# Projection matmuls in runs of twelve instead of six beside the attention of a hybrid decoder step

## The chip, the cores and the metric

The kernel runs on one core of a Trainium2 chip. The metric is the device time of one execution in microseconds (us), the median over runs. The names of the engines are those of the profile: PE (TensorE) multiplies, PEld is its weight load, DVE (VectorE) and ACT (ScalarE) do element work, POOL (GpSimd) does some of it too and issues gathers, and SP issues nearly all other transfers.

## The reference, cut to what matters

One layer of a decoder is applied to a prompt of 1024 tokens and to 8 samples of one token each:

```python
def adaln_project(x, c, w_ada, b_ada, w_in, b_in):
    mod = jax.nn.silu(c.astype(jnp.float32)) @ w_ada + b_ada
    shift, scale, gate = jnp.split(mod[:, None, :], 3, axis=-1)
    h = layer_norm(x) * (1.0 + scale) + shift
    split_points = np.cumsum(IN_SPLITS)[:-1].tolist()
    parts = jnp.split(h @ w_in + b_in, split_points, axis=-1)
    return parts, gate
...
        hm, (C_p, n_p, m_p) = mlstm_mixer(qm, km, vm, om, im, fm, m_norm_g[l], carry0, M_CHUNK)
        ha = nsa_prompt(qa, cmp_p, slc_p, win_p, ga, cmp_params, rel_bias)
        mix = jnp.concatenate([hm * jax.nn.silu(zm), ha * jax.nn.silu(za)], axis=-1)
        x_p = residual_out(x_p, mix, gate, w_out[l], b_out[l], ln_g[l], ln_b[l])
```

`h @ w_in` is the input projection: 1024 features in, 4384 out. Its outputs feed two groups of heads. The mLSTM group has 4 heads, each a chain of 8 chunks of 128 tokens. The attention group (NSA) has 8 query heads over 2 shared key/value heads and three branches: compressed blocks, selected blocks (16 of the 16 that a prompt has, so all that are causal) and a window of 512. For the samples the selected blocks come from a paged cache. The output projection follows, then a residual with a layer norm.

## The kernel before, in words

The order of all instructions is fixed when the program is built. Work is written as Python generators, called lanes. A lane emits instructions up to its next `yield`. `Lanes.run` then picks the lane of lowest rank whose operands are ready by a clock that the planner keeps (class `Plan`), and where none is ready it takes the one that is ready soonest. Each engine runs its own part of that fixed order and waits by semaphores.

The lanes that matter here, by rank:

- `all_scores` (rank 0) and `all_values` (rank 1): the attention of the prompt in 32 units (key/value head, block of 128 queries, pair of heads). The second key/value head goes through its query blocks from the longest to the shortest, so the last units are small. A unit has score products (PE: `sc<-kst,qs` and `sc<-kst,ql`), minima on DVE, exponentials on ACT, nine small steps in `factors` on DVE and ACT, scaling on ACT or DVE (`pp<-pp,ef`; `pa`, `pw` in the longer units), transposes on PE (`tp<-KA,pp`), copies on ACT or DVE (`pt<-tp`) and value products on PE (`oo<-pt,VT`, `oo<-pt,vcp`).
- `mlstm_prep`, `mlstm_head`, `mlstm_norm` (rank 2): per head two groups of four chunks. A chunk has three products (`sc<-vx,kw`, `sc<-cx,qm`, `sc<-vx,wt`); a group ends with a norm whose reciprocal root runs in small steps on POOL (`rs_v` to `mva`) and with four transposes (`tp<-KA,nd`).
- `sample_mlstm` (rank 5), `out_weights` (rank 6): after the attention and the third chain input of head 3, the state update of the samples (`Cst`), and then the output weights (`wof` times the gate, split into `woh` and `wol`). `output` needs all of these.
- `projections` (rank 9): 35 blocks of 128 output features, in the order of `order`. It is the last choice, and so it fills what the others leave free.

`in_proj` emits one block: three column chunks of 344 tokens, eight feature blocks `k` of 128 for each, three matmuls for each `k` (`mm<-hh,wh`, `mm<-hl,wh`, `mm<-hh,wl`). I call the three matmuls of one `k` a step, and number the steps through all blocks: block 28 has steps 673 to 696. After every second `k` it yields, and so six matmuls stand in a run:

```python
                if k % 2:
                    yield 0
```

The blocks of the mLSTM have a gate of their own. Block 29 (`qm`, head 3) is not begun before head 2 has ended, or before all attention values have, whichever is first:

```python
                if t:
                    yield from done("next%d" % (t - 1))
```

`flags` holds the names of what has ended; `PARTS` are the five flags "parts0" to "parts4" of the samples' selected rows and window rows. They are all set when some 304 of the 840 steps have been emitted.

Of the kernel before, what the change touches and what calls it, by code (L numbers as in the profile page):

```python
# [354 lines left out]
def build(ctx, tc, I, O, dbg=None):  # L355
# [5 lines left out]
    flags = lanes.flags  # L361
# [32 lines left out]
    def bank(tag, hold=False):  # L394

        def first():
            return min(idle(b) for b in range(8))
        if first() > plan.clock["PE"]:
            yield first
        while first() >= BIG:  # L400
            yield first
        return take(tag, hold)

    def free(*banks):

        for t in banks:
            held[next(b for b in range(8) if owner[b] is not None and owner[b].tensor.name == t.tensor.name)] = False
# [483 lines left out]
    def w_fetch(i):  # L891
        if i >= len(order):
            return
        name, t = order[i]
        wf = wfs[i] = R([128, 8, 128], "wf")
        if name == "g":
            dma(wf[:, :, 0:32], I["w_gate"].rearrange("p (k c) -> p k c", k=8))
        else:
            dma(wf.rearrange("p k c -> p (k c)"), I["w_blk"][BLOCKS.index((name, t))])

    def w_split(i):
        if i >= len(order):
            return
        wf = wfs.pop(i)
        wh, wl = [R([128, 8, 128], x, F32R) for x in ("wh", "wl")]
        n = 32 if order[i][0] == "g" else 128
        split(wh[:, :, 0:n], wl[:, :, 0:n], wf[:, :, 0:n])
        if n == 32:
            V.tensor_copy(wh[:, :, 32:64], fb(wl)[:, :, 0:32])
        whl[i] = (wh, wl)  # L910
# [10 lines left out]
    def done(*names):  # L921

        for n in names:
            if n not in flags:
                yield n
# [45 lines left out]
    def in_proj(i, evac, then=None):  # L971

        def later(wait, ev):
            yield wait
            yield from ev

        def last():
            yield from done(*["ev%d_%d" % (i, x) for x in range(3)])
            then()
        wh, wl = whl.pop(i)  # L980
        w_fetch(i + 1)
        for x, (c0, w) in enumerate(CH):
            if i == 0 and x:
                yield from done("h%d" % (x + 1), *(["hs"] if x == 2 else []))
            ps = yield from bank("mm", True)
            m = slice(c0, c0 + w)
            for k in range(8):
                if order[i][0] == "g":

                    T.matmul(ps[0:64, 0:w], wh[:, k, 0:64], hh[k][:, m], start=(k == 0), stop=False)  # L990
                    T.matmul(ps[0:64, 0:w], wh[:, k, 0:64], hl[k][:, m], start=False, stop=(k == 7))
                else:
                    T.matmul(ps[:, 0:w], wh[:, k], hh[k][:, m], start=(k == 0), stop=False)
                    T.matmul(ps[:, 0:w], wh[:, k], hl[k][:, m], start=False, stop=False)
                    T.matmul(ps[:, 0:w], wl[:, k], hh[k][:, m], start=False, stop=(k == 7))
                if k % 2:
                    yield 0
            ev = evac(ps[:, 0:w], c0, w)
            if ev:
                lanes.add(ER, later(next(ev), ev), "ev%d_%d" % (i, x))  # L1000
            free(ps)
            if x == 0:
                w_split(i + 1)
        if then:
            lanes.add(ER, last())
# [430 lines left out]
    PARTS = ["parts%d" % i for i in range(5)]  # L1436
# [449 lines left out]
    def projections():  # L1886
# [7 lines left out]
        for i, (name, t) in enumerate(order):  # L1894
            j = TI.get(name, 0) + t
            b, bh = BT[:, j:j + 1], BTH[:, j:j + 1]
            if name == "g":
                def evg(ps, c0, n):
                    low = H([32, 344], "gl")
                    S.activation(low, ps[32:64], AF.Identity, bias=bg)  # L1900
                    V.tensor_tensor(GT[:, c0:c0 + n], ps[0:32], low, op=ALU.add)
                yield from in_proj(i, evg)
                lanes.add(2, gates(), "gates")
            elif name == "qa":
                q = R([128, NT], "qt")
                yield from in_proj(i, plain(q, b))
                lanes.add(2, q_done(t, q), "q%d" % t)
                if t == 0:
                    lanes.add(4, ada(2))
            elif name == "za":  # L1910
# [10 lines left out]
                def z_done(t=t, z=z):  # L1921
                    V.tensor_copy(SZS[:, t], z[:, SEQ:NT])
                    store(gtd[4 + t], z[:, 0:SEQ], "z%d" % t)
                yield from in_proj(i, evz2, z_done)
            elif name in ("ck", "cv", "sk", "sv", "wk", "wv"):
                f = R([128, NT], "kvf")
# [544 lines left out]
```

## Time and profile before

| what | us |
|---|---|
| median of 3 runs | 1038.01 |
| their range | 1035.63 to 1041.17 |
| the profiled execution, its own time | 1039.46 |
| its span from first to last instruction | 1037.6 |
| PE busy | 959.7 |
| DVE busy | 717.2 |
| ACT busy | 530.2 |
| POOL busy | 286.5 |

Busy times are of the profiled execution. A matmul's recorded length overlaps that of the next one, so what one matmul costs is read from the distance between two starts. The granted clock is given as a share of full speed: 1.00 is 2.4 GHz, 0.50 is 1.2 GHz.

### The profile page before, as it was taken

To read this page: it belongs to the slowest core of one execution; us is meant where nothing else is said; L and a number is where in the kernel's file an instruction comes from. 1 tells how busy PE (TensorE), PEld (TensorE's weight loads), DVE (VectorE), ACT (ScalarE), POOL (GpSimd) and SP (SyncE) were. 2 spreads that over 40 slices of the span, in tenths; PEclk is the share of its full clock that TensorE was granted. 3 is DMA by queue.
4 is the path that set the end of the run, shared out by engine and by line. 5 is a ranking of instruction groups with operands and counts; after the bars stand their busy time and mean duration, and the time that the engine had idled before them with its cause. 6 is when DMAs were issued, how large, how long until landed. Compare 5 with 4: busy or idle time off the path is not lost.

```text
span 1037.6 us, 20058 instructions
## 1 busy us (share of the span) xinstructions
PE 959.7 (92%) x7338; PEld 864.9 (83%) x7338; DVE 717.2 (69%) x2266; ACT 530.2 (51%) x1329; POOL 286.5 (28%) x362
## 2 busy tenths in 40 slices
PE   4997899999999989999999999999999899989990
PEld 3786897989888889899999998899998889967780
DVE  4859864072323477789777788878784738999996
ACT  3557752143344656676667786666773321231111
POOL 6216423111453000110131001131012524253563
PEclk9988899999999989999999999999999989989996
DMA  8943419413698715311105111012102326479502
GB/s 329 408 189 117 148 70 361 151 50 118 221 326 286 216 55 165 111 57 37 47 11 157 29 47 38 25 36 74 47 33 85 113 65 191 142 264 362 168 22 81
DMA packets 85334, 141.42 MB, mean 136 GB/s; under 512 B 11657, under 2 KB 58286, under 8 KB 85108
## 3 DMA queue, kind: packets, MB, share of 16 engines
q1 hardware_dynamic: 76020, 106.59, 31.2%
q0 software_dynamic: 9216, 33.56, 9.0%
q8 instruction: 58, 0.95, 0.4%
q14 instruction: 40, 0.33, 0.1%
HBM read 117.73 MB, written 28.15 MB: 141 GB/s over the span
## 4 chain that ended last, share of the span: by engine, by line
PE 57%; DVE 11%; DMA 4%; issue 2%; POOL 2%; ACT 1%; POOLq 0%; SPq 0%; DVEq 0%; ACTq 0%
PE mm L308 27%; PE sc L308 13%; PE tp L308 9%; PE oo L308 7%; DVE xr L308 2%; DMA wof<-in_w_out 1%; DMA pgs<-in_cache_slc_kv,idx 1%; DVE smp L308 1%; DVE lnst L308 1%; DVE rs_t L308 1%; POOL wol L308 1%; DMA mg<-mgd 1%; DVE mixl L308 1%; DMA pgs<-in_cache_win_kv 1%; DVE rs_y L308 0%
## 5 line engine op out<-in xcount | busy, mean ns | idle before, releaser
L308 PE MATMUL mm<-hh,wh 128*128 128x344 f32 (+1 forms) x840 | 286.3, 341 | 0.0
L308 PE MATMUL mm<-hl,wh 128*128 128x344 f32 (+1 forms) x840 | 270.4, 322 | 0.0
L308 PE MATMUL mm<-hh,wl 128*128 128x344 f32 x816 | 262.6, 322 | 0.0
L308 POOL TENSOR_TENSOR wl<-wf,wh 128x1024 fp32r<-128x1024 f32 (+1 forms) x35 | 82.5, 2356 | 505.0 <-ACT wh L308 389.6
L308 PEld LDWEIGHTS mm<-hh,wh 128*128 128x128 f32 (+1 forms) x840 | 158.8, 189 | 12.1 <-issue 10.5
L308 PEld LDWEIGHTS mm<-hl,wh 128*128 128x128 f32 (+1 forms) x840 | 158.9, 189 | 0.7
L308 PEld LDWEIGHTS mm<-hh,wl 128*128 128x128 f32 x816 | 155.1, 190 | 0.0
L308 PE MATMUL oo<-pt,VT 128*64 128x128 f32 x1056 | 70.1, 276 | 0.0
L308 PE MATMUL sc<-kst,qs 128*128 128x448 f32 (+6 forms) x208 | 69.5, 343 | 0.3 <-DVE pt L308 0.3
L308 PE MATMUL sc<-kst,ql 128*128 128x448 f32 (+6 forms) x208 | 65.5, 325 | 0.0
L308 PEld LDWEIGHTS oo<-pt,VT 128*64 128x64 f32 x1056 | 58.1, 137 | 6.4 <-issue 5.2
L308 DVE COPY pt<-tp 128x512 f32<-128x512 f32 (+1 forms) x87 | 54.8, 645 | 9.9 <-PE tp L308 9.7
L308 ACT ACTIVATE pw<-pw,nbs 128x64 f32<-128x64 f32 (+2 forms) x112 | 54.6, 489 | 12.6 <-DVE tot L308 6.4
L308 ACT ACTIVATE pt<-tp 128x512 f32<-128x512 f32 (+1 forms) x73 | 39.8, 558 | 40.6 <-PE tp L308 40.4
L308 ACT ACTIVATE pa<-pa,nbs 128x384 f32<-128x384 f32 (+1 forms) x88 | 50.9, 580 | 14.6 <-DVE pa L308 12.4
L308 ACT ACTIVATE xh<-tp 128x512 fp32r<-128x512 f32 x64 | 38.0, 595 | 35.2 <-PE tp L308 34.9
L308 DVE TENSOR_TENSOR xl<-tp,xh 128x512 fp32r<-128x512 f32 x64 | 42.8, 679 | 14.3 <-ACT xh L308 14.0
L308 PE MATMUL tp<-KA,pgx 128*128 128x128 f32 x256 | 43.3, 293 | 2.8 <-ACT pgx L308 1.9
L308 ACT ACTIVATE ti<-sc,PKT 128x129 f32<-128x129 f32 x28 | 10.3, 369 | 67.3 <-DVE cx L308 67.3
L308 ACT ACTIVATE pp<-pp,nbs 128x64 f32<-128x64 f32 (+3 forms) x72 | 32.2, 449 | 22.7 <-DVE nbs L308 21.3
L308 PE MATMUL sc<-xl,w1h 128*128 128x256 f32 x128 | 38.3, 299 | 5.0 <-DVE xl L308 5.0
L308 PEld LDWEIGHTS sc<-kst,qs 128*128 128x128 f32 x208 | 39.8, 191 | 3.3 <-DVE pt L308 1.0
(506 smaller groups left out, 2285.0 us busy)
## 6 DMA issues: line engine op xcount, KB each, us to landing
wf<-in_w_blk SPq DMA_DIRECT2D x34, 512.0 KB
wada<-in_w_ada SPq DMA_DIRECT2D x24, 512.0 KB
wof<-in_w_out SPq DMA_DIRECT2D x16, 512.0 KB
xt<-in_x_prompt SPq DMA_DIRECT2D x8, 512.0 KB
pgs<-in_cache_win_kv SPq DMA_DIRECT2D x8, 512.0 KB
qf<-qtd SPq DMA_DIRECT2D x32, 128.0 KB
mix<-mxd SPq DMA_DIRECT2D x16, 256.0 KB
mix<-gtd SPq DMA_DIRECT2D x16, 256.0 KB
```

Source lines behind the costliest of these rows:

```text
L308: return f(*a, **kw)
```

## The change

One condition in `in_proj` changes:

```diff
-                if k % 2:
+                if k % 4 == 3 or k % 2 and not set(PARTS) <= flags:
                     yield 0
```

Until the five flags of the samples' rows are set, a block yields after every second `k` as before. From then on it yields after every fourth, so that a run has twelve matmuls. No instruction is added or removed on PE; the planner orders all engines' work anew from that point on.

On PE the first place where the order differs is step 306. `mm` is the projection, `sc` the score products of the second unit (the numbers are those of buffers):

```order
 L308 MATMUL mm_4233<-hl_842,wh_3726 128x344
 L308 MATMUL mm_4233<-hh_841,wl_3727 128x344
-L308 MATMUL sc_4243<-kst_3767,qs_4016 128x256
-L308 MATMUL sc_4243<-kst_3767,ql_4017 128x256
-L308 MATMUL sc_4249<-kst_3766,qs_4016 128x320
-L308 MATMUL sc_4249<-kst_3766,ql_4017 128x320
 L308 MATMUL mm_4233<-hh_921,wh_3726 128x344
 L308 MATMUL mm_4233<-hl_922,wh_3726 128x344
```

The four score products moved behind two more steps of the projection. From step 306 on PE has 97 runs of projection matmuls where it had 148, and 60 runs of value products where it had 63.

The second place is the end of the attention, on PE. Before, the last small units stand between steps 664 and 678, with one or two yields' worth of projection between them (`pp` are probabilities to transpose, `pt` transposed ones, `km` and `qm` inputs of mLSTM head 2):

```order
L308 MATMUL oo<-pt,vcp 64x128 x2
L308 MATMUL oo<-pt,VT 64x128 x4
L308 MATMUL sc<-qm,km 128x128 x4
L308 MATMUL tp<-KA,pp 128x128 x6
L308 MATMUL mm<-hh,wh 128x344
L308 MATMUL mm<-hl,wh 128x344
L308 MATMUL mm<-hh,wl 128x344
```

In the changed order the attention is later against the projection: by 10 to 20 steps at first, by 30 to 50 in its last third. Step 696 ends block 28 while six units' values, eight pairs of score products, five chunks of mLSTM head 2 and both of its norm's transposes (`nd`) are still to come. None of them has a projection step beside it until the attention's last value product. A piece from the middle:

```order
L308 MATMUL tp<-KA,nd 128x128 x4
L308 MATMUL sc<-kst,qs 128x128
L308 MATMUL sc<-kst,ql 128x128
L308 MATMUL tp<-KA,vm 128x128 x4
L308 MATMUL oo<-pt,vcp 64x128 x2
L308 MATMUL oo<-pt,VT 64x128 x8
L308 MATMUL tp<-KA,pp 128x128 x10
```

In all, 80 transposes, 60 value products, 16 score products, four products of `qm` and `km` and five chunks of three stand there in a row. A shorter row of the same kind stands at step 504, the end of block 20, with 36 transposes, 26 value products and 20 score products. Before, no such row stood at either step. The projection's steps between the end of the attention and the end of block 30 (`km`, head 3) were 66 and are 48.

The third place is DVE behind the attention. Before, the products and splits of two output weights stood ahead of the last chain input `km` (`mva`, `nd` and `qm` are the norm of head 2's second group, `vx` an input of head 3):

```order
L308 COPY vx<-tp 128x4x128
L308 TENSOR_TENSOR wof<-wof,gate 128x1024
L308 TENSOR_TENSOR wol<-wof,woh 128x1024 x2
L308 TENSOR_TENSOR mva<-mva,den 128x4
L308 TENSOR_SCALAR nd<-nd,mmv,mva 128x128 x4
L308 TENSOR_SCALAR qm<-tp,g_106 128x512
L308 TENSOR_SCALAR km<-mm,small 128x344 x3
```

Now they stand behind it, among the first steps of `sample_mlstm` (`lsg`, and `TR`, which holds its rows):

```order
L308 TENSOR_SCALAR km<-mm,small 128x344 x2
L308 COPY QS_136<-qm 128x8
L308 COPY QS_136<-km 128x8
L308 TENSOR_TENSOR kw<-tp,PKT 128x512
L308 MEMSET TR 128x512
L308 TENSOR_TENSOR wof<-wof,gate 128x1024
L308 TENSOR_TENSOR wt<-sc,wt 128x512
L308 COPY cx<-sc 128x129
L308 COPY nd<-sc 128x129
L308 SCALAR_TENSOR_TENSOR lsg<-GS 8x4
```

Here the weights' work moved behind `km`; a split (`wol`) stands a little later, and the other halves of both are on POOL. The norm of head 2's second group moved the other way, to before the attention's end.

## Rows read from the trace of the kernel before

**Rows 1.** Engines of the page: busy time, share of the span and instructions of each.

```profile
PE 959.7 (92%) x7338; PEld 864.9 (83%) x7338; DVE 717.2 (69%) x2266; ACT 530.2 (51%) x1329; POOL 286.5 (28%) x362
```

**Rows 2.** Busy time of each engine in stretches of the span: from and to (us), length, then PE, PEld, DVE, ACT and POOL with their instructions, the granted clock, the share of the DMA engines and GB/s.

```profile
450.00:500.00 50.00, 50.00 (x430) 47.02 (x429) 40.96 (x161) 33.43 (x101) 6.47 (x11) 1.00 0.15 47
...
700.00:750.00 50.00, 50.00 (x430) 46.15 (x430) 41.53 (x181) 36.48 (x114) 2.67 (x7) 1.00 0.18 58
...
800.00:850.00 50.00, 45.82 (x299) 45.28 (x298) 28.81 (x64) 11.39 (x22) 21.84 (x36) 0.93 0.27 87
850.00:900.00 50.00, 47.47 (x322) 43.40 (x321) 40.87 (x113) 14.33 (x30) 17.34 (x24) 0.93 0.48 139
900.00:950.00 50.00, 44.96 (x207) 37.54 (x206) 46.38 (x89) 13.68 (x19) 18.53 (x10) 0.93 0.89 291
```

**Rows 3.** The same view for one long stretch; then, for the same stretch, the group of the first of a step's three matmuls (busy us, mean ns | idle before).

```profile
400.00:750.00 350.00, 348.19 (x2965) 322.06 (x2965) 275.76 (x1131) 249.57 (x736) 50.22 (x122) 1.00 0.19 58
...
L308 PE MATMUL mm<-hh,wh 128*128 128x344 f32 x289 | 98.9, 342 | 0.0
```

**Rows 4.** PE in order of time inside that stretch: start us, recorded length, engine, operation, out<-in, count.

```profile
500.84 0.82 PE L308 MATMUL tp<-KA,pa 128*128 128x128 f32 x6
501.49 0.38 PE L308 MATMUL tp<-KA,pw 128*128 128x128 f32 x2
...
505.54 0.28 PE L308 MATMUL sc<-kst,qs 128*128 128x256 f32 x1
505.66 0.28 PE L308 MATMUL sc<-kst,ql 128*128 128x256 f32 x1
...
509.06 0.32 PE L308 MATMUL mm<-hh,wh 128*128 128x344 f32 x1
...
509.52 0.31 PE L308 MATMUL mm<-hh,wh 128*128 128x344 f32 x1
...
509.83 0.32 PE L308 MATMUL mm<-hh,wl 128*128 128x344 f32 x1
510.08 1.09 PE L308 MATMUL oo<-pt,VT 128*64 128x128 f32 x16
511.11 0.49 PE L308 MATMUL sc<-vx,kw 128*128 128x129 f32 x2
...
511.80 0.45 PE L308 MATMUL sc<-kst,qs 128*128 128x448 f32 x1
...
512.96 0.60 PE L308 MATMUL tp<-KA,km 128*128 128x128 f32 x4
513.31 0.41 PE L308 MATMUL mm<-hh,wh 128*128 128x344 f32 x1
513.56 0.32 PE L308 MATMUL mm<-hl,wh 128*128 128x344 f32 x1
```

**Rows 5.** PE rows with an idle time before them, and what ended it (in brackets).

```profile
387.45 0.76 PE L308 MATMUL tp<-KA,pp 128*128 128x128 f32 x5 [1.47 <-DVE pp L308]
...
425.65 0.66 PE L308 MATMUL tp<-KA,pp 128*128 128x128 f32 x2 [0.91 <-DVE pp L308]
...
794.61 0.60 PE L308 MATMUL sc<-mg,KA 128*9 128x512 f32 x1 [0.87 <-DMA mg<-mgd]
...
827.97 1.25 PE L308 MATMUL tp<-KA,nd 128*128 128x128 f32 x4 [4.18 <-DVE nd L308]
...
853.85 0.63 PE L308 MATMUL tp<-wd,on 8*128 8x32 f32 x2 [2.54 <-DVE d L308]
...
920.07 0.80 PE L308 MATMUL sc<-wol,mixh 128*128 128x512 f32 x1 [2.92 <-POOL wol L308]
```

**Rows 6.** Busy time of each engine and the granted clock in stretches of ten us (columns as in rows 2).

```profile
380.00:390.00 10.00, 8.53 (x64) 7.90 (x63) 8.32 (x38) 7.22 (x24) 2.50 (x3) 1.00 0.31 107
...
820.00:830.00 10.00, 5.82 (x32) 5.32 (x32) 6.42 (x9) 3.72 (x7) 6.76 (x15) 0.82 0.00 0
830.00:840.00 10.00, 10.00 (x57) 10.00 (x56) 1.59 (x4) 0.00 (x0) 2.21 (x1) 0.84 0.32 107
...
850.00:860.00 10.00, 7.46 (x59) 6.64 (x58) 5.58 (x31) 5.15 (x11) 1.93 (x5) 0.68 0.54 157
```

**Rows 7.** DVE and POOL in order of time behind the attention (columns as in rows 4).

```profile
790.75 0.28 DVE L308 TENSOR_SCALAR ao<-oo 128x128 f32<-128x128 f32 x1
...
814.63 2.42 POOL L308 TENSOR_TENSOR wl<-wf,wh 128x1024 fp32r<-128x1024 f32 x1
...
814.76 2.32 DVE L308 TENSOR_TENSOR den<-den,PKT 128x4 f32<-128x4 f32 x1
...
819.79 1.21 DVE L308 TENSOR_TENSOR wof<-wof,gate 128x1024 f32<-128x1024 f32 x1
820.92 2.44 DVE L308 TENSOR_TENSOR wol<-wof,woh 128x1024 fp32r<-128x1024 f32 x2
826.33 1.20 DVE L308 TENSOR_TENSOR mva<-mva,den 128x4 f32<-128x4 f32 x1 [2.98 <-POOL mva L308]
...
839.57 0.58 DVE L308 TENSOR_SCALAR km<-mm,small 128x344 f32<-128x344 f32 x1 [3.19 <-PE mm L308]
```

**Rows 8.** The chain that ended last, between the samples' state update and the output projection: start us, length, what.

```profile
900.00 0.69 DVE Cst L308
...
920.07 5.89 PE sc L308 x14
```

## The prediction

> **What bounds the kernel now.** I read the engines of the page first [rows 1]: PE is busy for 92% of the span, no other engine for more than 69%. An average hides stages, so next the stretches of the span [rows 2]. Between 400 and 800 us PE is full; from 800 to 900 it is not, and from 900 on DVE is the fullest engine (46.38 of 50 us) beside the output. The long stretch [rows 3] has PE at 348.19 of 350 us, while DVE is at 275.76. There the time is the sum of what PE does, and a mere change of order saves only what a border between two kinds of matmul costs. Then the idle times of PE [rows 5]: 1.47 and 0.91 us early in the attention, where probabilities come late from DVE, and behind the attention 0.87 (a load), 4.18 (the norm of head 2), 2.54 (the samples' chain) and 2.92 us (the last output weight). Last the chain [rows 8]: the samples' state update at 900.0 us, then output weights, then the output from 920.07 us. All that can be won lies in borders, in these gaps, and in the granted clock. It is 0.82, 0.84 and 0.68 in three stretches behind the attention [rows 6], where PE therefore ran part of the time at the lower of its levels (1.2 instead of 2.4 GHz).
>
> **The change, part by part.** No PE instruction comes or goes, so each term is a gap or a border.
>
> *Borders.* Runs of projection fall from 148 to 97, by 51. A border from transposes into a projection shows nothing: four transposes and the first matmul behind them take 512.96 to 513.56 us, 0.60, where four at 0.108 (six in 500.84 to 501.49) and a matmul at a third of a 0.46 step (509.06 to 509.52) would take 0.58 [rows 4]. A border into value products shows 0.25 us from the last matmul's start to the first product, against a third of a step, 0.15: 0.10. So 51 borders are worth between 0.4 us (0.007 each, the transposes' residue of 0.02 shared by three kinds) and 5.1 us (0.10 each). Both kinds occur, and I take the middle, 0.05: **-2.5**.
>
> *The early gaps.* The runs beside 387 and 425 us are twice as long, so a unit's DVE work has a step or two more of cover, 0.46 to 0.92 us. Against 1.47 and 0.91 that is between none (the next unit is late by the same) and all, 0 to -2.4. I take **-1**.
>
> *The norm of head 2.* Its transposes wait 4.18 us at 827.97 [rows 5]. The cause stands in [rows 7]: DVE is in a product and splits of output weights (`wof`, `wol`, 819.79 to 823.4), and the norm's last product `mva` waits for POOL until 826.33. The clock then falls: 0.82 over ten us is 3.6 us at half speed and 0.84 is 3.2 [rows 6], 6.8 in all, of which 5.2 lie behind the gap and so cost 2.6. The change puts this norm, and its four transposes, into the attention's end, and the weights' work behind `km`. The gap has nothing left to wait for, and its half clock goes with it. The 0.87 at 794.61 goes too: the 16 steps that now stand behind the attention's end (7.4 us) cover the load. Together 4.18 + 2.6 + 0.87 = **-7.7**. If the norm is late in its new place as well, as little as -0.9 is left. I take all of it, as POOL has little to do before 800 us (2.67 of 50 us in the last full stretch [rows 2]).
>
> *The short row at step 504.* 36 transposes at 0.108, 26 value products at 0.128 (the trace counts two rows for one of the order: 16 in 1.03 us from 510.08) and 20 score products at 0.12 at most (505.54 to 505.66) are 9.6 us of PE without projection [rows 4]. What DVE has to do for such work: in the long stretch 289 steps at 0.46 are 133 of 350 us, so 217 us of other PE work went with 275.76 us of DVE, 1.27 to 1 [rows 3]. 9.6 us want 12.2 of DVE, so PE idles 2.6 us if DVE is never idle, and nothing if the units in hand last. Bounds 0 and 4, I take **+2**.
>
> *The long row at step 696.* 80 transposes (8.7 us), 60 value products (7.7), 16 score products (1.9), four of `qm` and `km` (0.5) and five chunks at 0.69 (511.11 to 511.80; 3.5) are 22.3 us of PE [rows 4]. This is the heart of the forecast. Before, projection filled every wait there; now none can, as block 29 waits for head 2 or for the last value. At 1.27 the row wants 28.3 us of DVE: 6.0 us idle if DVE is always busy. It is not when PE waits for it, since a unit goes to and fro between PE, DVE, ACT and POOL: between 380 and 390 us, the one place before with idle PE of this kind, DVE was busy 8.32 of 10 us [rows 6]. At that share the row lasts 34.1 us, 11.8 idle. Bounds 6.0 and 11.8, and I take a share of 0.89, halfway: 31.8 us, **+9.5**.
>
> *The clock behind it.* At 380 to 390 us PE was busy 8.53 of 10 and the clock stayed at 1.00; at 850 to 860 it was busy 7.46 and the clock was 0.68, 6.4 us at half speed, which cost some 3 [rows 6]. The row's busy share, 22.3 of 31.8, is 0.70, nearer to the second. But parts of the row are fuller than others, and what PE does at half speed while DVE is the bound costs nothing. Between 0 and 5, I take **+2.5**.
>
> *DVE and POOL behind the attention.* 1.21 us for `wof` and 1.22 for one `wol` [rows 7] now stand in the samples' chain, whose end sets the output's start; 12 more steps of projection come ahead of the last `Cst` product, which other waits held there before. Against that, the products of head 3's denominators (`den`) move behind it. One such instruction took 2.32 us beside POOL's `wl` of 2.42, from 814.63 and 814.76 to the same end [rows 7]; it has four columns. The Trainium skill, "SBUF — State Buffer", "Who interferes with whom", says why that can be: DVE and GpSimd share a pair of ports under an exclusive lock. The trace agrees in this pair of rows; were the rule to hold for each of the moved weights, the sum would move by up to two POOL instructions, 4.8 us, either way by who comes first. From the rows alone: two instructions of 1.2 us more and about as much less, bounds -4 and +4, I take **0**.
>
> **Sum.** -2.5 - 1 - 7.7 + 2 + 9.5 + 2.5 + 0 = +2.8 us. The profiled execution took 1039.46 us, 1.45 above the median, so 1042.3 in its terms, and **1040.8** for the median, from 1038.0. About 0.5%, 5.2 us, is what a measurement of this kernel can tell from no change; the forecast lies inside, 1032.8 to 1043.2.
>
> **The rivals.** *Faster: the rows are hidden.* If DVE runs ahead of PE before step 696, so that the row stays at its lower idle time of 6.0 and the one at 504 at none, if the clock does not fall, and borders are worth 4 and the early gaps 1.5, the sum is -4 - 1.5 - 7.7 + 6.0 = -7.2: 1031 us. For it speaks that DVE has 17% to spare in the last full stretch (41.53 of 50) [rows 2]; against it, that it has to have worked units ahead whose buffers PE has yet to free. The Trainium skill, "Perfetto Trace Analysis", "Matmul Optimizations", would lead there: it asks for matmuls back to back in batches, as the engine scales its power with use. In this trace the clock is 1.00 all through the mixed work of [rows 3], so longer runs have nothing to give there; what is to be had lies where PE idled.
>
> *Slower: DVE bounds the last attention units.* All filler is used up before the units that it was meant to fill. If the row at 696 goes at the DVE share of 380 to 390 us (11.8 us idle), that at 504 costs 4, the clock falls behind both (5), and borders and early gaps give 1.5 and 0.5, the sum is 11.8 + 4 + 5 - 7.7 - 2 = +11.1: 1049 us. It decides once idle time and clock of the two rows pass 5.2 + 2.5 + 1 + 7.7 = 16.4 us; the forecast has 14. For it speaks that small units carry as many small DVE steps as large ones for less PE work, so that 1.27 may be low for the last; against it, that mLSTM work lies in the row as well. In a sentence of the skill against this change ("Perfetto Trace Analysis", "Optimization Strategy"), stretches in which different engines are the most contended are better interleaved; that is what the smaller runs did.
>
> *Only a new order.* The row costs what the three gaps gave, as projection left over from the row fills later waits, and borders alone count: -2.5 from the median, 1035.5 us, no change.
>
> **How the numbers follow.** The forecast has 0.33, the mere order 0.14, the slower rival 0.31, the faster one 0.22. A small part of the forecast's own spread lies above 1043.2, so faster is 0.22, same 0.45, slower 0.33. The predicted time is the forecast's, 1041. The range reaches past the centres of both outer rivals, since half of each lies beyond its centre, 0.26 together: 1030 to 1050 leaves out 0.08 below and 0.11 above.
>
> **What would show it.** In the changed trace: PE's idle time from step 696 to the last value product (9.5 us here, 6 or 12 by the rivals) with `pp` or `pt` as what ended it; DVE's share there, near 0.89; the granted clock in and behind the row; no idle time of 4 us before an `nd` transpose, and full clock where `km` ends; a shorter row with 2 us at step 504; first matmul of the output near 920 + 2.8 = 923 us. I am wrong if the last units come earlier against the projection on the chip than in the written order, which cannot be as PE goes in order, or, more likely, if the samples' chain, not PE, sets the output's start: then the row's idle time is given back behind it.

## The result and the profile after

The changed kernel takes 1054.22 us (median of 4 runs, 1051.51 to 1057.32) against 1037.70 for the kernel before (4 runs): 1.0146 times as long, 95% interval 1.0122 to 1.0169. It is slower by some 16 us, and the forecast of 1041 and its range to 1050 both missed it. The profiled execution took 1055.94 us with a span of 1054.1, against 1039.46 and 1037.6.

First the engines of the page of after, beside [rows 1]:

```profile
PE 958.2 (91%) x7338; PEld 861.4 (82%) x7338; DVE 702.8 (67%) x2244; ACT 537.4 (51%) x1347; POOL 293.2 (28%) x366
```

PE is busy for as long as before. So the 16 us are time in which PE waits. Where, the starts of its instructions tell. Three stretches cover the program from the first place where the order differs: from the first matmul behind step 306 to the last projection matmul, from there to the first output product, and from that to the end of the last output product.

| stretch | before | after | difference |
|---|---|---|---|
| behind step 306 to the last projection matmul | 370.41 to 913.73: 543.3 | 369.80 to 913.07: 543.3 | 0.0 |
| to the first output product | 913.91: 0.2 | 927.14: 14.1 | +13.9 |
| to the end of the output products | 1013.58: 99.7 | 1028.89: 101.8 | +2.1 |

Outside these stretches the two differ little: the changed kernel comes to the first 0.6 us earlier and takes 1.3 us longer behind the last. The whole stretch in which runs have twelve matmuls instead of six comes out even within some 1 us. (The four score products that moved stand just ahead of it before and inside it in after; from the start of step 306 itself, 368.59 and 369.22, it is 545.14 against 543.85.) The loss lies behind it, where no projection is left. Busy time of each engine in after (columns as in [rows 2]), two full stretches of the attention, the long row at step 696, the end of the projection, and the 13 us behind it:

```profile
450.00:500.00 50.00, 50.00 (x413) 47.41 (x413) 40.93 (x176) 36.98 (x116) 6.47 (x11) 1.00 0.18 53
700.00:750.00 50.00, 49.60 (x418) 46.27 (x416) 38.64 (x164) 36.69 (x112) 4.71 (x7) 1.00 0.14 44
...
783.00:816.00 33.00, 25.43 (x254) 21.32 (x252) 25.54 (x119) 22.06 (x74) 6.25 (x32) 1.00 0.05 13
...
900.00:913.00 13.00, 13.00 (x85) 12.92 (x84) 12.06 (x39) 3.42 (x7) 5.63 (x4) 1.00 0.56 165
913.00:926.40 13.40, 0.58 (x5) 0.29 (x3) 12.91 (x22) 3.63 (x5) 8.55 (x4) 0.60 0.46 183
```

In the last row PE does 0.58 us of work in 13.40, while DVE is busy for 12.91 with only 22 instructions. PE's rows with an idle time (as [rows 5]), in the long row and behind the projection:

```profile
791.93 0.44 PE L308 MATMUL tp<-KA,pp 128*128 128x128 f32 x2 [1.58 <-DVE wt L308]
798.60 0.63 PE L308 MATMUL tp<-KA,pp 128*128 128x128 f32 x4 [0.89 <-ACT pp L308]
800.47 1.10 PE L308 MATMUL tp<-KA,pp 128*128 128x128 f32 x6 [0.82 <-DVE vx L308]
807.43 1.60 PE L308 MATMUL tp<-KA,pp 128*128 128x128 f32 x10 [2.62 <-ACT pp L308]
810.91 1.06 PE L308 MATMUL tp<-KA,pp 128*128 128x128 f32 x6 [0.44 <-ACT pp L308]
812.50 0.44 PE L308 MATMUL oo<-pt,vcp 128*64 128x128 f32 x4 [0.53 <-ACT pt L308]
813.85 1.06 PE L308 MATMUL tp<-KA,pp 128*128 128x128 f32 x6 [0.47 <-ACT pp L308]
...
926.33 1.16 PE L308 MATMUL tp<-KA,nd 128*128 128x128 f32 x4 [12.82 <-DVE nd L308]
...
933.12 0.80 PE L308 MATMUL sc<-woh,mixh 128*128 128x512 f32 x1 [2.64 <-ACT woh L308]
936.09 0.80 PE L308 MATMUL sc<-wol,mixh 128*128 128x512 f32 x1 [2.17 <-POOL wol L308]
```

One wait of 12.82 us stands out. It is for `nd`, the normed second group of head 3, the last norm of all. The kernel before waited 1.72 us inside the same four transposes:

```profile
912.27 0.84 PE L308 MATMUL tp<-KA,nd 128*128 128x128 f32 x3 [1.72 <-DVE nd L308]
```

PE goes in order, so the output products behind them wait too. The reciprocal root of this one norm does not run on POOL, as that of the others does, but on DVE (`E = V if h == 3 and g else G` in `mlstm_norm`), so the whole norm is a chain on DVE. What DVE and POOL did in that time in after:

```profile
911.41 5.27 POOL L308 TENSOR_TENSOR wof<-wof,gate 128x1024 f32<-128x1024 f32 x2 [6.08 <-DMA wof<-in_w_out]
916.64 4.91 POOL L308 TENSOR_TENSOR wol<-wof,woh 128x1024 fp32r<-128x1024 f32 x2
...
903.99 0.69 DVE L308 TENSOR_TENSOR Cst<-sc,Cst 128x512 f32<-128x512 f32 x1
...
908.16 0.15 DVE L308 SCALAR_TENSOR_TENSOR den<-nd 128x4 f32<-128x4 f32 x1
...
911.78 0.62 DVE L308 TENSOR_SCALAR MXS<-tp,g 128x8 f32<-128x8 f32 x4
912.32 2.15 DVE L308 SCALAR_TENSOR_TENSOR tz<-tz,zv 128x344 f32<-128x344 f32 x1
914.50 2.54 DVE L308 SCALAR_TENSOR_TENSOR to<-to,tz 128x344 f32<-128x344 f32 x1
916.97 2.31 DVE L308 TENSOR_SCALAR rs_v<-mva 128x4 f32<-128x4 f32 x1
919.31 2.26 DVE L308 TENSOR_SCALAR rs_y<-rs_v 128x4 int32<-128x4 int32 x1
921.61 0.17 DVE L308 TENSOR_SCALAR rs_v<-rs_v 128x4 f32<-128x4 f32 x1
```

Four GpSimd instructions stand in a row from 911.41 to 921.55, on the output weights, 2.5 us each. Beside them DVE finishes four instructions, each about when one of GpSimd's ends: `tz` and `to`, which take 0.50 and 0.52 us elsewhere, and two steps of the norm's reciprocal root on 128x4 numbers. The next one, at 921.61, when GpSimd is done, takes 0.17. The four `MXS` products at 911.78, whose input `tp` comes from PE's transposes, are not held: they take 0.62 us together beside GpSimd's first. The kernel before had these steps earlier:

```profile
906.13 2.42 POOL L308 TENSOR_TENSOR wof<-wof,gate 128x1024 f32<-128x1024 f32 x1 [12.52 <-DMA wof<-in_w_out]
...
891.30 2.33 DVE L308 SCALAR_TENSOR_TENSOR den<-nd 128x4 f32<-128x4 f32 x1
...
903.65 0.16 DVE L308 TENSOR_SCALAR rs_v<-mva 128x4 f32<-128x4 f32 x1
903.84 0.17 DVE L308 TENSOR_SCALAR rs_y<-rs_v 128x4 int32<-128x4 int32 x1
...
905.70 0.16 DVE L308 SCALAR_TENSOR_TENSOR mva<-rs_t,rs_y 128x4 f32<-128x4 f32 x1
905.78 0.51 DVE L308 SCALAR_TENSOR_TENSOR tz<-tz,zv 128x344 f32<-128x344 f32 x1
906.33 2.61 DVE L308 SCALAR_TENSOR_TENSOR to<-to,tz 128x344 f32<-128x344 f32 x1
```

The reciprocal root was over at 905.86, 0.27 us before GpSimd's first weight product began. Of what follows, only `to` and one of the `nd` products met GpSimd; `den` had met another instruction of GpSimd's at 891.30, 19 us ahead of the transposes. That is possible because the first part of the norm (`den` to `mva`, 13 instructions) stood ahead of the last state update `Cst` before, and stands behind it in after. The last `Cst` itself is later too: it starts at 903.99 instead of 900.00 [rows 8], 9.1 instead of 13.7 us ahead of the last projection matmul. No run below takes that part by itself.

### The profile page after: what moved, and what is told of

It is laid out like the page before. It is cut to its first block, busy times and chain, and to the rows that moved or that the text cites. A ratio compares the mean times of both kernels' runs of the same rounds, so it can differ in the third digit from the quotient of the medians.

```text
span 1054.1 us, 20080 instructions
## 1 busy us (share of the span) xinstructions
PE 958.2 (91%) x7338; PEld 861.4 (82%) x7338; DVE 702.8 (67%) x2244; ACT 537.4 (51%) x1347; POOL 293.2 (28%) x366
## 4 chain that ended last, share of the span: by engine, by line
PE 55%; DVE 12%; issue 3%; ACT 3%; DMA 2%; POOL 2%; POOLq 0%; ACTq 0%; DVEq 0%
PE mm L308 27%; PE sc L308 12%; PE tp L308 9%; PE oo L308 7%; DVE xr L308 2%; DVE rs_t L308 1%; DMA pgs<-in_cache_slc_kv,idx 1%; DVE smp L308 1%; DVE lnst L308 1%; POOL wol L308 1%; ACT pp L308 1%; DMA pgs<-in_cache_win_kv 1%; ACT xr L308 1%; DVE rs_y L308 1%; POOL wl L308 0%
## 5 line engine op out<-in xcount | busy, mean ns | idle before, releaser
L308 PE MATMUL mm<-hh,wh 128*128 128x344 f32 (+1 forms) x840 | 281.7, 335 | 0.0
L308 ACT ACTIVATE pp<-pp,nbs 128x64 f32<-128x64 f32 (+3 forms) x72 | 32.2, 450 | 25.3 <-DVE nbs L308 25.1
L308 PE MATMUL sc<-xh,w1h 128*128 128x256 f32 x128 | 42.8, 334 | 0.0
```

Source lines behind the costliest of these rows:

```text
L308: return f(*a, **kw)
```

## The experiments

All were made to find out where the 16 us come from. In what follows, "wait" is PE's idle time before the last four `nd` transposes. "Stretch" is the time of DVE's small instructions between the last `Cst` and those transposes that is over their shortest length in any of the runs (those over by 0.6 us or more). Some runs were on chips on which step 306 starts 12 to 20 us later for every kernel profiled there and the kernel before takes 1052.7 to 1055.5 us. So ratios are against the kernel before on the same chip, and stretches are counted from the first matmul behind step 306. One more caution: what stands behind the last output product took 24.0 us before and 25.3 in after, but 13 to 21 in several of the runs, so a longer output is not a loss of the same size.

**GpSimd's weight work left out.**

```diff
-            sooner((V, 1.2), (G, 2.3)).tensor_tensor(w, w, og["gate"], op=ALU.mult)
+            if (e := sooner((V, 1.2), (G, 2.3))) is G and "smlstm" in flags and "mn31" not in flags:
+                plan.note("POOL", "tensor_tensor", (w, w, og["gate"]), {})
+            else:
+                e.tensor_tensor(w, w, og["gate"], op=ALU.mult)
```

The split has the same condition, with a copy on ACT in its place.

> Left out here, with every other instruction in the order of the changed kernel: GpSimd's products with the gate and splits for the output weights that come between the end of the samples' state update and the end of head 3's last norm (two products, and the splits that the plan gives it there; the splits become plain copies on ACT). Theory A (these weights' work on GpSimd stretches VectorE's small instructions of the norm beside it, four of which took 2.15 to 2.54 us in the changed kernel): the four fall to 0.5, 0.5, 0.15 and 0.15 us, the wait of the norm's transposes for nd falls from 12.8 us to about 4, and the whole comes to 1043 to 1048 us. Theory B (the norm is late because of its place in VectorE's order and because the weights' transfers are late, GpSimd has no part in it): the four stay over 2 us or the wait stays over 10 us, and the time stays within 2 us of the changed kernel's 1054.

Measured: 1.0072 (1.0045 to 1.0100). PE's waits, and DVE, in this run:

```profile
915.75 1.16 PE L308 MATMUL tp<-KA,nd 128*128 128x128 f32 x4 [4.93 <-DVE nd L308]
...
909.65 0.51 DVE L308 SCALAR_TENSOR_TENSOR tz<-tz,zv 128x344 f32<-128x344 f32 x1
910.20 0.52 DVE L308 SCALAR_TENSOR_TENSOR to<-to,tz 128x344 f32<-128x344 f32 x1
910.63 0.16 DVE L308 TENSOR_SCALAR rs_v<-mva 128x4 f32<-128x4 f32 x1
910.83 0.17 DVE L308 TENSOR_SCALAR rs_y<-rs_v 128x4 int32<-128x4 int32 x1
```

Theory A holds: the same instructions in the same order take 0.51, 0.52, 0.16 and 0.17 us, and the wait falls by 7.89 to 4.93 us. The stretch in after was 7.95. Half of the loss goes with GpSimd's work; half is left. (Weights that are left out cannot be late either: the output took 99.6 us here instead of 101.8. The same edit in the kernel before, at the end of this section, gains nothing measurable.)

**The weights on DVE instead.** `sooner((V, 1.2), (G, 2.3))` becomes `V` between the end of the state update (`smlstm`) and the end of the norm (`mn31`).

> The changed kernel with the products and splits of the output weights between the end of the samples' state update and the end of head 3's last norm given to VectorE (1.2 us each) instead of to GpSimd (2.4 us each), nothing left out. Theory A (GpSimd beside VectorE stretches the norm): VectorE does three such instructions more, 3.6 us, but its small instructions fall from 2.2 to 2.5 us back to 0.15 to 0.5, so the transposes' wait falls from 12.8 to about 8 us and the time to 1046 to 1051. Theory B (VectorE's order alone): the norm ends 3.6 us later still, 1056 to 1059.

Measured: 1.0173 (1.0121 to 1.0226), no gain. The wait fell to 9.34 and the stretch to 2.13, near what theory A expected, but the time, 1056.5 us, lies where theory B put it. Inside the output PE waited 12.25 us instead of 4.81: 6.66 for `woh` and `wol`, and 4.49 near its end for `mixl`, the low part of the output's input, which DVE makes. The work that GpSimd gave up was not free on DVE.

**One part of the change at a time.** Runs of twelve up to the last value product only, and behind it only:

```diff
-                if k % 4 == 3 or k % 2 and not set(PARTS) <= flags:
+                if k % 4 == 3 or k % 2 and (not set(PARTS) <= flags or "values" in flags):
```
```diff
-                if k % 4 == 3 or k % 2 and not set(PARTS) <= flags:
+                if k % 4 == 3 or k % 2 and "values" not in flags:
```

> Runs of twelve matmuls only until the last value product of the attention; behind it runs of six as before. The long row at step 696 stays, the part behind the attention has the short runs. Theory A (the loss is made behind the projection by the order of norm, state update and output weights; the attention part costs nothing): the end of the projection lies within 3 us of both kernels'; since the plan of the tail still has head 3's norm behind the last state update and three weight products in a row on GpSimd, the output starts late again and the time is 1044 to 1056. Theory C (longer runs behind the attention are the loss): 1036 to 1040.

> Runs of twelve matmuls only behind the last value product; the attention is word for word that of the kernel before, so there is no long row. Theory A (the loss is made behind the projection): the plan again puts head 3's norm behind the last state update, with six weight products in a row on GpSimd, so the time is 1046 to 1058 although the attention is unchanged. Theory D (the row of attention without projection is the loss): 1035 to 1040.

Measured: 1.0176 (1.0132 to 1.0219) and 1.0134 (1.0092 to 1.0177). Both alone lose as much as the whole change, so the loss is not a sum over its parts. In the first, which has the long row, step 306 to the end of the projection took 543.4 us, the same as before, and behind the attention the runs are short: theory C falls (its time, 1057.3 us, is also 1.3 above theory A's range). In the second, whose attention is that of the kernel before, it took 536.9, 6.4 less, and yet all was lost again: theory D falls. Here six weight products stand in a row on GpSimd (second run: POOL, DVE, PE):

```profile
907.56 14.53 POOL L308 TENSOR_TENSOR wof<-wof,gate 128x1024 f32<-128x1024 f32 x6 [14.53 <-PE mm L308]
...
907.60 2.38 DVE L308 SCALAR_TENSOR_TENSOR rs_y<-rs_t,rs_y 128x4 f32<-128x4 f32 x1
910.01 2.27 DVE L308 TENSOR_TENSOR rs_t<-rs_y 128x4 f32<-128x4 f32 x1
912.31 2.27 DVE L308 TENSOR_TENSOR rs_t<-rs_t,rs_v 128x4 f32<-128x4 f32 x1
914.62 2.27 DVE L308 SCALAR_TENSOR_TENSOR mva<-rs_t,rs_y 128x4 f32<-128x4 f32 x1
...
922.63 1.16 PE L308 MATMUL tp<-KA,nd 128*128 128x128 f32 x4 [12.64 <-DVE nd L308]
```

Again about one DVE instruction gets through for each of GpSimd's. The stretch is 12.74 us and the wait 12.64.

**Holding the weight work back until the norm is through.**

```diff
         yield from done(after[-1])
+        if ks[0] in (6, 0):
+            yield from done("mn31")
```

> The changed kernel, in which the products and splits of the output weights 6, 7 and 0 to 3 wait until head 3's last norm is in VectorE's order; nothing left out. Theory A (the loss is GpSimd's weight work beside that norm): the norm's transposes wait 3 to 6 us instead of 12.8, the first split that the output needs ends 8 to 12 us sooner, and the time is 1040 to 1047. Theory B (the norm and the transfers are late anyway): no gain, 1052 to 1058, since the weights start later still.

> The same hold in the kernel before. There the norm was ahead of most of the weights' work. Theory A: to, nd and MXS fall from 2.61, 3.15 and 4.73 us to 0.5, 1.1 and 0.4, and the weights begin 3 to 4 us later, so the time stays at 1034 to 1041. Theory B: the later start of the weights moves the output by as much, 1040 to 1043.

> Runs of twelve only behind the attention, with the hold. Without the hold this order ended its projection some 6 us sooner than the kernel before (from step 306 on) and gave more than that back at the norm (12.64 us of wait) and at the output's first split. Theory A: the wait falls to 3 to 5 us and the 6 us stay, 1033 to 1041. Theory E (the output's start hangs on the weights' transfers and products, not on the norm): the weights, begun later, are late, 1044 to 1050.

Measured: 1.0204 (1.0168 to 1.0239), 1.0110 (1.0076 to 1.0144) and 1.0086 (1.0057 to 1.0115). All three expectations of theory A failed. The wait for `nd` did fall, to 8.0 us in the first and to none above 2 us in the other two. But the weights then came late: PE waited 15.6, 16.5 and 18.9 us inside the output, which took 115 to 120 us instead of 99.7. Of these waits 10.0, 14.1 and 12.6 us were for `woh` and `wol`, the rest for `mixl`. In the first:

```profile
955.10 0.80 PE L308 MATMUL sc<-woh,mixh 128*128 128x512 f32 x1 [4.28 <-ACT woh L308]
```

**The norm behind the weights**, so that PE can begin the output without it: `mlstm_norm` of head 3, second group, begins with `yield from done("w7")`.

> The changed kernel, in which head 3's last norm does not begin before output weight 7 is ready, so that its transposes stand behind the first output products on PE; nothing left out. Theory A (PE, which goes in order, stands before the output because that norm is stretched beside GpSimd's weight work, and the weights queue behind it on VectorE): the first output product comes 8 to 14 us sooner against the end of the projection, and the time is 0.3 to 1.0% above or below the kernel before on the same chip instead of 1.5% above. Theory E (the weights themselves are late, whatever the norm does): the ratio stays at 1.012 or more.

> The same edit in the kernel before, where the norm was ahead of the weights and the output waited 1.72, 0.39 and 2.92 us. Theory A: up to 4 us gained, ratio 0.995 to 1.003. Theory E: ratio 0.998 to 1.003 as well; this run only tells whether the edit by itself is worth something.

> Runs of twelve only behind the attention, with the later norm. Theory A: the 6 us by which this order ends the projection sooner stay, ratio 0.990 to 0.999. Theory E: ratio 1.008 or more, as with the hold.

> The changed kernel itself on the chip of these runs, so that the ratios of the other three have it beside them: every theory expects 1.012 to 1.017, 12 to 14 us of wait before the norm's transposes, and the same times from step 306 on as in its first profile within 1 us.

Measured: 1.0198 (1.0168 to 1.0228), 1.0169 (1.0135 to 1.0204), 1.0136 (1.0104 to 1.0168), and 1.0163 (1.0133 to 1.0193) for the changed kernel itself, with a wait of 12.80 us and 543.3 us from step 306 to the end of the projection once more. The output did begin 0.2 us behind the projection, as theory A said, and then waited 15.6 to 18.2 us in its middle, so that the times are those of theory E (and the kernel before lost 1.7%, which neither expected). In the kernel before the longest wait was for the norm (5.93 us), with more for the part of the input that hangs on it; in the other two it was for a weight, `woh` (10.51 and 6.91 us), although the weights now stood ahead of the norm. Between the state update and the output both chains, the norm's and the weights', are needed within a few us; the hold of the weights made them late, and with the later norm they were late all the same in two of three kernels.

**The place of the norm.** First the kernel before, its runs of six untouched, with the norm put behind the last `Cst`; then two kernels with the norm's first part put ahead of the last two `Cst` products; then the changed kernel with runs of six from the last chain on. The flag `Cend` is set behind the last `Cst`, `nb` behind the first part of that norm:

```diff
+        if h == 3 and g:
+            yield from done("Cend")
```
```diff
             yield [vb]
+            if h == 3:
+                yield from done("nb")
```
```diff
-                if k % 4 == 3 or k % 2 and not set(PARTS) <= flags:
+                if k % 4 == 3 or k % 2 and (not set(PARTS) <= flags or "qs3" in flags):
```

> The kernel before, with runs of six as they were, in which head 3's last norm does not begin before the last state update of the samples is in VectorE's order; four weight products then stand in a row on GpSimd beside it. Theory F (the place of the norm behind the state update is the loss): the transposes wait 8 to 14 us for nd and the ratio is 1.006 to 1.015, although no run is longer. Theory G (the place does not matter, the longer runs cost elsewhere): the wait stays under 5 us, ratio 0.997 to 1.004.

> The changed kernel, in which the last head's two state products wait until the first part of that norm is in VectorE's order. Theory F: the wait for nd falls from 12.8 to under 6 us and the ratio to 0.998 to 1.008. Theory G: ratio 1.012 to 1.018 as before the edit.

> The changed kernel with runs of six again once the last chain's input is ready (end of block 30, step 744); the attention keeps its runs of twelve and its long row. The plan puts the norm ahead of the last state update by itself. Theory F: the wait for nd is under 6 us, ratio 0.998 to 1.008, so attention with long runs costs nothing measurable. Theory G: 1.010 or more.

> Runs of twelve only behind the attention, with the norm's first part ahead of the last state products. That order ended the projection 6 us sooner after step 306. Theory F: what is won there stays, ratio 0.990 to 1.001. Theory G: 1.008 or more.

Measured: 1.0114 (1.0067 to 1.0160), 1.0128 (1.0082 to 1.0174), 1.0171 (1.0126 to 1.0215) and 1.0065 (1.0038 to 1.0091). The first is the loss made by hand in a kernel without a single longer run:

```profile
918.49 10.01 POOL L308 TENSOR_TENSOR wof<-wof,gate 128x1024 f32<-128x1024 f32 x4 [9.54 <-DMA wof<-in_w_out]
...
923.84 2.38 DVE L308 TENSOR_SCALAR rs_v<-mva 128x4 f32<-128x4 f32 x1
926.26 2.26 DVE L308 TENSOR_SCALAR rs_y<-rs_v 128x4 int32<-128x4 int32 x1
928.56 2.27 DVE L308 TENSOR_SCALAR rs_v<-rs_v 128x4 f32<-128x4 f32 x1
...
937.22 1.16 PE L308 MATMUL tp<-KA,nd 128*128 128x128 f32 x4 [10.81 <-DVE nd L308]
```

The other three say that the place alone is not all. With the norm's first part ahead, its second part still met GpSimd: a stretch of 5.74, 8.51 and 1.68 us, and waits of 9.23, 7.58 and 2.0 twice. Theory F was right in the first and missed in the others; the last of them lies between F and G.

**Both removed**, and the control:

> The changed kernel with the norm's first part ahead of the last state products and, left out, GpSimd's products and splits of the output weights between the end of the state update and the end of the norm (the splits become copies on ACT). If stretch and place are the whole loss: no instruction of the norm over 1 us, a wait for nd under 4 us, ratio 0.996 to 1.004. If a third cause is left: 1.006 or more.

> The kernel before with the same work left out (one product and one split lie in that window). Its two stretched instructions (4.1 us together) fall to 0.5 and 1.1 us, its wait for nd of 1.72 us goes; the output still waits for its weights: ratio 0.994 to 1.000.

Measured: 1.0058 (1.0038 to 1.0078) and 0.9988 (0.9959 to 1.0017). No instruction is stretched in either; the wait is 3.64 us in the first, whose ratio falls between the two that were expected, nearer to "a third cause". What is left is 0.7% beside the control. In the first run's profile, which is of its slowest execution (1067.16 us, median 1061.37), PE waits 5.86 us for `woh`, 1.64 for `wol` and 2.90 for `mixl` inside the output, and its beginning runs at a granted clock of 0.50 (1.2 GHz), where the control runs at 1.00 (2.4 GHz). The two lines are of the first run and of the control:

```profile
935.00:952.00 17.00, 8.77 (x21) 6.16 (x22) 15.75 (x26) 4.19 (x5) 8.59 (x3) 0.50 0.66 221
...
925.00:945.00 20.00, 18.08 (x79) 14.20 (x78) 18.61 (x24) 7.44 (x9) 10.12 (x5) 1.00 0.86 278
```

So something more is there: the lateness of the output weights, and PE work at the lower clock beside those waits. It was not taken apart further.

The time from the last `Cst` to the first `nd` transpose, with the stretch (and DVE's own weight work in it) taken off, puts most of the runs together:

| run | last `Cst` to `nd` | stretch | DVE's weights | rest |
|---|---|---|---|---|
| kernel before | 9.6 | 2.1, and 2.0 behind the first transpose | 0 | 7.5 at most, as PE was not waiting yet |
| changed | 21.6 | 7.95 | 1.2 | 12.5 |
| GpSimd's work left out | 13.7 | 0 | 1.2 | 12.5 |
| twelve in the attention only | 25.2 | 9.4 | 0 | 15.7, with 3.4 of DVE idle |
| twelve behind the attention only | 23.6 | 12.74 | 0 | 10.9 |
| norm behind, in the kernel before | 24.2 | 11.45 | 1.2 | 11.6 |
| norm ahead, in the changed kernel | 15.4 | 5.74 | 0 | 9.7 |
| norm ahead, twelve behind the attention only | 10.1 | 1.68 | 0 | 8.4 |
| norm ahead, and GpSimd's work left out | 9.8 | 0 | 0 | 9.8 |

The rest is 11 to 12.5 us where the norm is behind the last `Cst` and DVE does not idle, and 8 to 10 where its first part is ahead. Of the 12.0 us between the first two rows, the stretch has 5.8, the rest 5.0 and DVE's weight product 1.2. The stretch is the larger and the more variable part.

## Why the prediction was wrong

The step that failed is "DVE and POOL behind the attention", which stood in the sum at 0 between -4 and +4. It measured +16: 13.9 us ahead of the output and 2.1 in it, the latter with more waiting for weights (4.81 us against 3.31). The row that shows the mechanism was among those read (`den`, 2.32 us beside POOL's `wl`, [rows 7]), and the prediction said that the `den` block moves behind the last `Cst`. But the sum priced two DVE instructions of 1.2 us more and about as much less, and the meeting with POOL, set beside it, at two POOL instructions, 4.8 us. What the order put beside each other was a chain of some 25 dependent small DVE instructions, with `tz` and `to` among them, and four POOL instructions in a row; four of DVE's took 2.15 to 2.54 us. The bound should have been one POOL instruction for each that POOL has in a row, 10.1 us for the four here. That the chain is so long is due to this one norm's root being on DVE. And the chain was taken to end where it ended before, without asking what PE has queued behind the `nd` transposes: the whole output. A reading went wrong on the way: 920.07 us, taken for the output's start, is where it went on after its last wait [rows 5]. Its first product stands at 913.91, right behind the projection, so there was no slack ahead of it; in after it came at 927.14, 13.2 us later, not the 2.8 that were forecast.

Point by point, the rest of the sum, which ran to the end of the projection:

- *Borders* (-2.5): nothing was gained. Idle times over 0.3 us from step 306 to the end of the projection add up to 12.2 us before and 13.2 after, and both take 543.3 us, though the second runs less of it at half clock (below). What PE spent without waiting did not fall.
- *The early gaps* (-1): 1.37 us at 396.96 and 0.89 at 514.85 stand in place of 1.47 and 0.91 [rows 5], so 0.1 us was gained.
- *The norm of head 2* (-7.7): right. The 4.18 and the 0.87 us are gone, and the granted clock is 1.00 from 816 to 850 us, where it was 0.82 and 0.84 [rows 6]. Not in the sum was a new wait of 1.51 us at 874.05, for `vb` of the samples' chain.
- *The short row at step 504* (+2): no idle time of 0.3 us in it, its lower bound.
- *The long row at step 696* (+9.5): right in kind, with `pp` as what ended most waits. The seven rows above add up to 7.35 us, inside the bounds of 6.0 and 11.8. But the sizes behind these bounds were off and balanced by luck: DVE was busy 25.54 of 33.0 us, a share of 0.77 and so below both that were taken (1 and 0.83), as the waits were DVE's and ACT's in turn; and the row held 25.4 us of PE work, not 22.3, so DVE's work was 1.0 to 1 of PE's, not 1.27. (Halfway between the two shares would have been 0.92 and 8.6 us, not 0.89 and 9.5.)
- *The clock behind it* (+2.5): 1.00 in the row and up to 874 us, so 0. Behind the wait for `vb` alone did it fall to 0.50 before the projection ended, for 3.4 us.

Taken together these steps came to 0.0 instead of +2.8 (to -1.3, counted from step 306 itself), and what was gained there paid for the row. To the end of block 30, which takes in the rows, the longer runs do cost a little: from step 306 to the first matmul behind step 744 the ten profiles with twelve in the attention took 472.1 to 474.2 us, the nine with six 469.0 to 470.8. The slower rival had the sign and nearly the size (1049), by a mechanism that did not decide: the attention's last units cost 7.35 us of the 16.4 that it asked for, and the run with long runs only in the attention ended its projection at 543.4. The run with long runs only behind the attention shows that a loss of this size needs no such row. The last sentence of the prediction came near the place ("if the samples' chain, not PE, sets the output's start") but expected only that the row's idle time would be given back there.

The Trainium skill, "SBUF — State Buffer", "Who interferes with whom", says that the pair of ports that DVE and GpSimd share is an exclusive lock, and that where a DVE instruction in a 2-port mode contends with GpSimd, the one that issues first holds the pair for the whole instruction while the other blocks fully. If that holds for the small instructions here, the price of one is what is left of GpSimd's. The durations in the traces agree: 0.16 and 0.17 us became 2.26 to 2.38 beside products of 2.3 to 2.7, and 0.16 again with those left out. Which mode an instruction was in, no run here shows.

That some 8 of the 16 us go with GpSimd's work, and the stretch with them, is shown (the run without it, and its control). That the norm's place alone makes a loss of this size, by bringing the stretch with it, is shown in the kernel before. That the rest comes from the norm's place, the later `Cst` and late weights is argued from the waits, not shown; what puts the weights late is open. Why the longer runs move the norm behind the last `Cst` was not settled either: the runs with only one half of the change do it too, and that of runs of six from the last chain on does not.

## What to carry to other kernels

A change of order is not over where the code that it touches ends: look at what stands together at the seam behind it, on the engines that are full there. Where a chain of small dependent DVE instructions can fall beside wide GpSimd instructions, price it at one GpSimd instruction for each that GpSimd has in a row, and ask what PE has queued behind the chain's end. Moving one of two chains that are both due at the same point can make it late without freeing the other, as the hold and the later norm showed here.

## What was not expected of the hardware

Beside a row of GpSimd instructions on 128x1024 numbers, DVE went forward at about one instruction each: 4 beside 4 (stretch 7.95 us), 6 beside 6 (12.74 us). Those that were held took as long with 4 columns as with 344. Not all were: in the changed kernel four `MXS` products that read the transposes' result `tp` took 0.62 us together beside GpSimd, as they did with GpSimd's work left out. And the long row, with 7.35 us of idle time in 33, kept the granted clock at 1.00, while in ten us of the kernel before with 7.46 busy it was 0.68 [rows 6].
